# A two-block transformer in split fp32: one beginning, the expert loads, the window attention and four other places put in another order, and all weight splits ranked 60 instructions later

## The chip, the cores and the metric

The kernel runs on one core of a Trainium2 chip. The metric is the device time of one execution in microseconds (us). The engines are TensorE (PE in the profile, its weight loads PEld), VectorE (DVE), ScalarE (ACT), GpSimd (POOL) and SyncE (SP), which here issues most of the loads.

## What is computed

The reference is a transformer of two blocks on 256 tokens of width 1024, in fp32. Cut to its structure:

```
block 1:  x = LN_in(x)
          for l in 0, 1:
              m = MLA (8 heads) | differential (4) | forgetting (4) attention of x @ w_in[l]
              x = LN1(alpha * x + m @ w_out[l])
              x = LN2(alpha * x + MoE_l(x))     # 16 experts of width 512, 4 groups, top 2
block 2:  for i in 0, 1:
              x = x + FFN1_i(rms(x)) / 2
              x = x + (SSD scan and pooling mixer if i == 0 else sliding-window attention with sinks)
              x = x + cross-attention of rms(x) to a memory of 256 rows
              x = x + FFN2_i(rms(x)) / 2
```

## The kernel before

Tokens lie in two tiles of 128 rows, t = 0 and 1, in the rows tile `res`. A weight GEMM is made of three products of fp32r halves: each operand is split in a high part (an ACT copy to fp32r) and a low part (a DVE subtraction), and `mm3` (L479 to 485) adds high*high, high*low and low*high. `gemm_t` (L1618) does the same for transposed outputs, most of all in the FFN.

Weights come through the class `Stream` (L82 to 191). Its plan, fixed in `plan` and `plan2` (L331 to 477), is a list of 1 MB units that SP loads in that order into a ring of 7 stage tiles, and of pieces that are split from a unit into a ring of 6 piece tiles (L161 the ACT copy, L162 the DVE subtraction). Expert weights are `raw` units: used as plain fp32 and not split, they go to both rings in turn, or to a named free slot. `take` hands out a piece, `release` frees it and splits what comes next, `hold` stops the splitting ahead of a key, and `go` lifts that. Which instruction stands where on each engine is decided by the scheduler of the tile framework, which ranks instructions by the order in which the program traces them, and by priorities; `after(...)` lets an instruction stand behind named others.

**Block 1.** The beginning (`block1`, L775) loads x, small vectors, tables and the first units; `LayerNorm` (L194) normalizes rows (`ln_norm`, L570), and `x_t` (L534) transposes a tile on PE (L541) and splits it. There, gain and bias of the first LayerNorm are applied per column while PSUM is evacuated; the rows get theirs later (`ln_gain`, L598). `ln_full` (L584) does both on the rows, with gain and bias spread over the partitions. `mixer` (L818) runs five blocks of `w_in`, then the attentions; `fox_decay` (L1071) is the forgetting attention's decay. `memory` (L1715) prepares the normalized memory (L1724, L1729) for the cross-attention's keys and values, whose GEMM (`memory_gemm`, L1745) is done in quarters inside the MoE.

**MoE** (`moe`, L1208). Experts are taken in pairs, pr = 0 to 7, two experts side by side in the PE array. A pair has gate and up (`gate_or_up`, L1341, matmul L1352), activation (L1362, 1363), transposes (`tr`, L1369), down (L1386); `gather(g)` (L1306) collects the rows of two pairs, and `scatter` (L1401, residual add L1403) returns a pair's rows by a matmul with `ptr`. The tail after pair 7 is the last scatter, LN2 (L592 to 596) and the second half of the memory GEMM (L1758). A branch (L1410) handles overflow.

**Block 2.** `xattn` (L1805): queries (`queries`, L1821: squares, reciprocal root L506 to 518, scaling L1829 and L1831, transposes L1837, scores L1846), `attend` (L1849), output GEMM `xo`. `swa` (L1894), the window attention: first the keys and values of `qkv`, then `queries(0, 1)` and `queries(1, 1)` (L1946 to 1971, transposes L1967), then `attend(0)` and `attend(1)` (L1986) on eight score blocks (L1980, L1982; softmax from L2000, transposes L1150, L1168 out products), with the output GEMM `swo` behind. `ssd` (L2038): pooling input (L2059), rows (L2114), `bn` (L2145), the chain over heads (L2157 to 2181, prob L2163 and L2166, PE L2175), and z in eight blocks (L2189).

## Time and profile before

| | us |
|---|---|
| median of 3 runs (lowest, highest) | 2002.53 (2001.20, 2002.54) |
| the profiled execution's own time | 2002.3 |
| its span in the profile | 2000.5 |
| PE busy | 1935.0 (97%) |
| DVE busy | 1127.0 (56%) |
| ACT busy | 866.9 (43%) |
| DMA moved | 453.39 MB, mean 227 GB/s |
| mean granted clock of PE | 0.986 |

The span is the time from the first to the last instruction of one execution; the execution's own time has 1.8 us more around it. Busy time is a share of the whole span and says nothing about where an engine waits. PE's matmul ends are modelled, so a busy PE can still be at half its clock; the column PEclk of the windows table shows the clock granted in a stretch, where 1.00 is 2.4 GHz and 0.50 is 1.2 GHz. A row of the waits names the line that waited, after the arrow the engine, tile and line that it waited for, then the sum, the count and the longest in us.

### The profile page before, as it was taken

How to read it: one execution, taken by the hardware profiler on the slowest of the kernel's cores; microseconds unless marked ns; L12 is line 12 of the kernel's file. 1: busy time of each engine (PE TensorE's matmuls, PEld its weight loads, DVE VectorE, ACT ScalarE, POOL GpSimd, SP SyncE). 2: the span in 40 equal slices, each digit the busy share in tenths (PEclk: the TensorE clock that was granted, in tenths of full speed). 3: DMA queues.
4: the chain of work that ended last, by engine and by line, in shares of the span. 5: the costliest groups of instructions: out<-in, count | busy, mean ns of one | idle time of the engine just before them, and what ended most of it. 6: DMA issues, size and time to landing. Idle time of an engine off the chain costs nothing.

```text
span 2000.5 us, 28009 instructions
## 1 busy us (share of the span) xinstructions
PE 1935.0 (97%) x11069; PEld 1458.6 (73%) x11069; DVE 1127.0 (56%) x2211; ACT 866.9 (43%) x1539; POOL 58.0 (3%) x119
## 2 busy tenths in 40 slices
PE   6999999999999998899999899999999999999999
PEld 6776433367864333599988887899989986778998
DVE  7775122167751221656579775655665567766554
ACT  6563110136631101455466555644454455556443
POOL 1110000000100000000001000000000000000000
PEclk9999999999999999999999999999999997999999
DMA  8456999973569999855564353455555543335550
GB/s 290 145 203 229 397 419 420 421 256 123 206 236 403 420 421 421 300 187 181 186 202 137 132 219 109 163 190 190 190 200 186 182 165 137 127 99 175 190 190 22
DMA packets 176044, 453.39 MB, mean 227 GB/s; under 512 B 11120, under 2 KB 106844, under 8 KB 149148
## 3 DMA queue, kind: packets, MB, share of 16 engines
q1 hardware_dynamic: 172044, 435.55, 59.1%
q0 software_dynamic: 3856, 15.91, 2.2%
q8 instruction: 91, 1.49, 0.3%
q14 instruction: 53, 0.43, 0.1%
HBM read 446.19 MB, written 5.24 MB: 226 GB/s over the span
## 4 chain that ended last, share of the span: by engine, by line
PE 56%; DMA 5%; DVE 3%; ACT 2%; issue 0%; POOL 0%; DVEq 0%; SPq 0%; POOLq 0%; ACTq 0%
PE mm L1623 7%; PE mm L1625 7%; PE mm L1624 7%; PE accb L485 5%; PE accb L484 5%; PE accb L483 4%; PE acca L485 4%; PE acca L484 4%; PE acca L483 4%; DMA piece<-in_exp_w_gate_dram 2%; DMA piece<-in_exp_w_down_dram 1%; DMA stage<-in_exp_w_down_dram 1%; DMA stage<-in_exp_w_up_dram 1%; DVE piece L162 1%; PE mm L1876 1%; PE mm L541 1%
## 5 line engine op out<-in xcount | busy, mean ns | idle before, releaser
L162 DVE TENSOR_TENSOR piece<-stage,piece 128x1024 fp32r<-128x1024 f32 (+3 forms) x439 | 513.8, 1179 | 240.9 <-ACT piece L161 239.3
L161 ACT ACTIVATE piece<-stage 128x1024 fp32r<-128x1024 f32 (+3 forms) x439 | 444.5, 1021 | 343.8 <-PE mm L1625 204.4
L1352 PE MATMUL mm<-stage,m 128*64 128x512 f32 x512 | 221.8, 595 | 0.0
L1352 PE MATMUL mm<-piece,m 128*64 128x512 f32 x480 | 215.1, 596 | 2.0 <-DMA piece<-in_exp_w_up_dram 2.0
L1623 PE MATMUL mm<-m,piece 128*128 128x256 f32 x736 | 207.0, 281 | 2.3 <-DVE m L2189 2.3
L1624 PE MATMUL mm<-m,piece 128*128 128x256 f32 x736 | 206.7, 281 | 0.0
L1625 PE MATMUL mm<-m,piece 128*128 128x256 f32 x736 | 206.6, 281 | 0.0
L1623 PE MATMUL mm<-xh,piece 128*128 128x256 f32 x576 | 163.1, 283 | 0.0
L1625 PE MATMUL mm<-xh,piece 128*128 128x256 f32 x576 | 163.0, 283 | 0.0
L1624 PE MATMUL mm<-xl,piece 128*128 128x256 f32 x576 | 162.9, 283 | 0.0
L484 PE MATMUL accb<-piece,m 128*128 128x512 f32 (+1 forms) x364 | 144.3, 397 | 0.0
L485 PE MATMUL accb<-piece,m 128*128 128x512 f32 (+1 forms) x364 | 143.7, 395 | 0.5 <-DVE m L493 0.5
L483 PE MATMUL accb<-piece,m 128*128 128x512 f32 (+1 forms) x364 | 143.1, 394 | 0.9 <-ACT m L950 0.7
L1623 PEld LDWEIGHTS mm<-m,piece 128*128 128x128 f32 x736 | 139.4, 189 | 4.6 <-issue 3.0
L1624 PEld LDWEIGHTS mm<-m,piece 128*128 128x128 f32 x736 | 139.3, 189 | 1.9 <-issue 0.3
L1625 PEld LDWEIGHTS mm<-m,piece 128*128 128x128 f32 x736 | 139.4, 189 | 0.0
L483 PE MATMUL acca<-piece,m 128*128 128x512 f32 (+1 forms) x348 | 138.2, 398 | 0.2
L485 PE MATMUL acca<-piece,m 128*128 128x512 f32 (+1 forms) x348 | 137.2, 396 | 0.5 <-DVE m L493 0.5
L484 PE MATMUL acca<-piece,m 128*128 128x512 f32 (+1 forms) x348 | 137.7, 396 | 0.0
L1352 PEld LDWEIGHTS mm<-stage,m 128*64 128x64 f32 x512 | 65.1, 137 | 76.4 <-issue 73.8
L1623 PEld LDWEIGHTS mm<-xh,piece 128*128 128x128 f32 x576 | 110.4, 192 | 1.3
L1624 PEld LDWEIGHTS mm<-xl,piece 128*128 128x128 f32 x576 | 110.4, 192 | 1.2
(567 smaller groups left out, 3535.8 us busy)
## 6 DMA issues: line engine op xcount, KB each, us to landing
stage<-in_ffn_wi_dram SPq DMA_DIRECT2D x88, 1024.0 KB, 5.5
stage<-in_ffn_wo_dram SPq DMA_DIRECT2D x44, 1024.0 KB, 5.4
stage<-in_exp_w_down_dram SPq DMA_DIRECT2D x38, 1024.0 KB, 18.6
stage<-in_exp_w_up_dram SPq DMA_DIRECT2D x34, 1024.0 KB, 11.2
stage<-in_exp_w_gate_dram SPq DMA_DIRECT2D x30, 1024.0 KB, 18.5
piece<-in_exp_w_gate_dram SPq DMA_DIRECT2D x30, 1024.0 KB, 17.9
piece<-in_exp_w_up_dram SPq DMA_DIRECT2D x30, 1024.0 KB, 15.0
piece<-in_exp_w_down_dram SPq DMA_DIRECT2D x26, 1024.0 KB, 16.8
```

What stands on the lines that cost most here:

```text
L161: nc.scalar.activation(wh, src, AF.Copy)
L162: nc.vector.tensor_tensor(wl, src, wh.bitcast(F32), op=OP.subtract)
L483: nc.tensor.matmul(out, ah, bh, start=first, stop=False)
L484: nc.tensor.matmul(out, ah, bl, start=False, stop=False)
L485: return nc.tensor.matmul(out, al, bh, start=False, stop=last)
L541: self.moved = nc.tensor.transpose(p[:, k * P:(k + 1) * P], src[:, 4 * q + k:D:8], self.c["ident"])
L1352: mm = nc.tensor.matmul(o[64 * k:64 * k + 64, :], x[:, j, s:s + CAP], w[k][:, jj, :], start=(j == 0), stop=(j == 7))
L1623: nc.tensor.matmul(out, wh[:, j, :], hi[:, j, :], start=(j == 0), stop=False)
L1624: nc.tensor.matmul(out, wh[:, j, :], lo[:, j, :], start=False, stop=False)
L1625: nc.tensor.matmul(out, wl[:, j, :], hi[:, j, :], start=False, stop=(j == 7))
L1876: nc.tensor.matmul(po[:, k * P:(k + 1) * P], v[:, mc, h * 256 + cc * P:h * 256 + (cc + 1) * P], pt[t][:, (2 * h + mc) * P:(2 * h + mc + 1) ...
```

## The change

It joins several edits.

1. *Splits.* Both instructions of a weight split are traced under a priority of −60, so that the scheduler ranks them as if they came 60 instructions later. A raw unit in the piece ring waits only for the splits before it, and no longer for raw pieces.
2. *Beginning.* The first LayerNorm and LN1 apply gain and bias to the rows at once (`ln_full`), so `ln_norm`, `ln_gain`, the gain columns of both, and the bias branch of `x_t` are gone. Their vectors are loaded as rows, those of the first LayerNorm right after the first tile of x; the first unit of `w_in` is issued ahead of the small loads. Splitting starts with two pieces after tile 0's copies, the rest after tile 1's LayerNorm. The router's weights need no scaling any more.
3. *MoE.* Four expert halves that are not first in the stream are loaded early into slots that are free: up of expert 0 and both downs; before, two gate halves were. Gathers copy without gain; `gather(1)` comes at the end of pair 1, `ptr` in pair 2, gathers 2 and 3 in pairs 3 and 5. A pair's down stands behind its last up matmul. The second half's memory weights are loaded ahead of the next block's; in the tail splitting begins again only after LN2's tile 0 (two pieces) and tile 1.
4. *Mixer.* `fox_decay` stands after the MLA attention instead of after the third block of `w_in`; the differential heads' rotation goes from POOL to DVE.
5. *Cross-attention.* The query GEMM of t = 1 is finished bank by bank with its norm, transposes and scores come after the last query product, and the output weights are held until the last normalization of the attention.
6. *Window attention.* The order is queries 0, keys and values, attend 0, queries 1, attend 1.
7. *SSD.* Evacuations L2059, L2114 and L2145 go from DVE to ACT; z is copied by ACT and multiplied by DVE in SBUF.

The core of the diff:

```diff
+        self.ws = Stream(nc, self.sp, self.wp, self.slot, lambda: self.tc.high_priority(-60))
...
+            with self.later():
+                nc.scalar.activation(wh, src, AF.Copy)
+                nc.vector.tensor_tensor(wl, src, wh.bitcast(F32), op=OP.subtract)
...
-        self.units.append(dict(ap=ap, a=a, b=b, left=1, tile=None, ring=ring, slot=slot, first=len(self.pieces)))
+        first = max((p["n"] + 1 for p in self.pieces if not p.get("raw")), default=0)
+        self.units.append(dict(ap=ap, a=a, b=b, left=1, tile=None, ring=ring, slot=slot, first=first))
...
+            slots = {("up", 0, 4): "m4", ("down", 0, 0): "xl", ("down", 1, 0): "m1", ("down", 0, 4): "xh"}
...
+                    if n == NSTAGE + NPIECE - 2:
+                        early("down", 1, 0)
+                        early("down", 0, 4)
+            mem(1024 * l + 512)
...
-            mem(1024 * l + 512)
...
-                self.plan_cols("qkv", w, 1024, 512)
-                self.plan_cols("qkv", w, 0, 1024)
+                for c0 in (0, 1024, 512):
+                    self.plan_cols("qkv", w, c0, 512)
...
-        self.rsqrt1(r, mv[:, 1:2], 0)
-        nc.vector.scalar_tensor_tensor(v, v, r, gb[1], op0=OP.mult, op1=OP.add)
+        sqrt = self.rsqrt1(r, mv[:, 1:2], 0)
+        return sqrt, nc.vector.scalar_tensor_tensor(v, v, r, gb[1], op0=OP.mult, op1=OP.add)
...
+            if l == 0 and bi == 0:
+                with self.after(*norm.half):
+                    ws.go(2)
+                with self.after(norm.last, norm.sqrt):
+                    ws.go()
...
-                nc.scalar.activation(x[:, j0, :], p[:, 0:256], AF.Identity, scale=g1[:, j0:j0 + 1], bias=b1[:, j0:j0 + 1])
-                at = nc.vector.tensor_scalar(x[:, j0 + 1, :], p[:, 256:512], g1[:, j0 + 1:j0 + 2], b1[:, j0 + 1:j0 + 2],
-                                             op0=OP.mult, op1=OP.add)
+                nc.scalar.activation(x[:, j0, :], p[:, 0:256], AF.Copy)
+                nc.vector.tensor_copy(x[:, j0 + 1, :], p[:, 256:512])
...
-            prev = []
+            prev = [state["last"]]
...
-                if pr == 8:
-                    with self.after(state["silu"], state["tr"]):
-                        ws.go(4)
-            if pr == 0:
-                gather(1)
-            if pr == 1:
+            if pr == 2:
...
+            with self.after(*nxt.copied):
+                ws.go(2)
...
+        ws.hold("xo")
+        self.gemm_rows("xq", 8, lambda k: (hi[:, k, :], lo[:, k, :]), acc=rows(), done=chain, cuts=(2,), by_bank=True)
+        with self.after(self.last_mm):
+            for x in steps:
+                next(x, None)
...
+        with self.after(at[3]):
+            ws.go()
...
-        queries(0, 1)
-        queries(1, 1)
-        attend(0, bias, "xl")
+        attend(0, bias, "xl")
+        queries(1, 1)
...
-                nc.vector.tensor_scalar(u[:, t, b * 512:(b + 1) * 512], acc[t], r[:, t:t + 1], None, op0=OP.mult)
+                nc.scalar.activation(u[:, t, b * 512:(b + 1) * 512], acc[t], AF.Copy, scale=r[:, t:t + 1])
...
-            nc.vector.tensor_tensor(zs[:, ch, :], p[:, 0:256], rrow, op=OP.mult)
+            nc.scalar.activation(zs[:, ch, :], p[:, 0:256], AF.Copy)
+            nc.vector.tensor_tensor(zs[:, ch, :], zs[:, ch, :], rrow, op=OP.mult)
```

What this does to the order of instructions is shown at three places, before and after. A row has line, operation, out<-in and shape, and a count where it repeats. Lines of the changed kernel are its own.

DVE at the end of the second layer's MoE, before. L489 splits the last pair's rows, L1403 adds a scatter to the residual, L162 is a weight split, and L592 begins LN2.

```order
L489 TENSOR_TENSOR xh<-acca,xh 128x512 x2
L1403 SCALAR_TENSOR_TENSOR res<-res,mm 128x512 x4
L489 TENSOR_TENSOR xh<-accb,xh 128x512 x2
L1403 SCALAR_TENSOR_TENSOR res<-res,mm 128x512
L162 TENSOR_TENSOR piece<-stage,piece 128x1024 x2
L1403 SCALAR_TENSOR_TENSOR res<-res,mm 128x512
L162 TENSOR_TENSOR piece<-stage,piece 128x1024 x2
L1403 SCALAR_TENSOR_TENSOR res<-res,mm 128x512 x2
L592 BN_STATS bnst<-res 128x6 x3
```

The same place after, where L493, L1367, L167 and L577 are those lines.

```order
L493 TENSOR_TENSOR xh<-acca,xh 128x512 x2
L1367 SCALAR_TENSOR_TENSOR res<-res,mm 128x512 x4
L493 TENSOR_TENSOR xh<-accb,xh 128x512 x2
L1367 SCALAR_TENSOR_TENSOR res<-res,mm 128x512 x4
L577 BN_STATS bnst<-res 128x6 x3
L578 BN_AGGR bnmv<-bnst 128x2
L577 BN_STATS bnst<-res 128x6
L579 SCALAR_TENSOR_TENSOR res<-res,bnmv,gv 128x1024
```

The two pairs of weight splits no longer stand among the residual adds.

DVE in the first cross-attention, before: the query norm of t = 0, from the variance of the four heads (L512) to the scaling of the products (L1831).

```order
L162 TENSOR_TENSOR piece<-stage,piece 128x1024
L514 RECIPROCAL sq_t<-sq_t 128x4
L162 TENSOR_TENSOR piece<-stage,piece 128x1024
L515 TENSOR_TENSOR sq_v<-sq_v,sq_t 128x4
L516 TENSOR_TENSOR sq_v<-sq_v,sq_t 128x4
L162 TENSOR_TENSOR piece<-stage,piece 128x1024
L517 TENSOR_SCALAR sq_v<-sq_v 128x4
L518 TENSOR_TENSOR xss<-sq_v,sq_t 128x4
L162 TENSOR_TENSOR piece<-stage,piece 128x1024
L1829 TENSOR_SCALAR xss<-xss,rms_r 128x4
L162 TENSOR_TENSOR piece<-stage,piece 128x1024
L1831 TENSOR_TENSOR m_12447<-acca,xss 128x512 x2
```

After, L516 to L522 are the same helper, and L1795 is the scaling.

```order
L516 TENSOR_SCALAR sq_v<-xssq 128x4
L518 RECIPROCAL sq_t<-sq_t 128x4
L519 TENSOR_TENSOR sq_v<-sq_v,sq_t 128x4
L520 TENSOR_TENSOR sq_v<-sq_v,sq_t 128x4
L521 TENSOR_SCALAR sq_v<-sq_v 128x4
L522 TENSOR_TENSOR xssq<-sq_v,sq_t 128x4
L1793 TENSOR_SCALAR xssq<-xssq,rms_r 128x4
L1795 TENSOR_TENSOR m_12376<-acca,xssq 128x512 x2
```

Between the links of the chain stood five splits (L162), and none stands there now.

PE in the window attention, before: the last query products (L483 to L485), the first scores (L1980, L1982) and the transposes of the second half's queries (L1967).

```order
L484 MATMUL accb<-piece,m_16266 128x512
L485 MATMUL accb<-piece,m_16267 128x512
L1980 MATMUL acca<-m_16394,m_16392 128x128 x2
L1982 MATMUL acca<-m_16394,m_16392 128x256 x2
L1980 MATMUL acca<-m_16394,m_16392 128x128 x2
L1982 MATMUL acca<-m_16394,m_16392 128x256
L1967 MATMUL mm<-ident,xh 128x128 x8
L1982 MATMUL acca<-m_16394,m_16392 128x256
L1980 MATMUL acca<-m_16394,m_16392 128x128
L1982 MATMUL acca<-m_16394,m_16392 128x256
L1980 MATMUL acca<-m_16394,m_16392 128x128
L1982 MATMUL acca<-m_16394,m_16392 128x256
```

After, L1961 and L1963 are the scores, L486 to L488 the query products of the second half, and L1948 the transposes of the keys.

```order
L1948 MATMUL mm<-ident,m_16334 128x128 x8
L487 MATMUL accb<-piece,m_16207 128x512
L488 MATMUL accb<-piece,m_16208 128x512
L486 MATMUL accb<-piece,m_16207 128x512
L1961 MATMUL acca<-m_16335,m_16333 128x128 x2
L1963 MATMUL acca<-m_16335,m_16333 128x256 x2
L487 MATMUL accb<-piece,m_16207 128x512
L488 MATMUL accb<-piece,m_16208 128x512
L1961 MATMUL acca<-m_16335,m_16333 128x128
L1963 MATMUL acca<-m_16335,m_16333 128x256
L1961 MATMUL acca<-m_16335,m_16333 128x128
L1963 MATMUL acca<-m_16335,m_16333 128x256
```

The scores now stand between products of the second half's queries; before, all products stood ahead of them.

## Rows read from the trace of the kernel before

**Rows 1.** page part 1: engine, busy us, share of span, instructions

```profile
PE 1935.0 (97%) x11069; PEld 1458.6 (73%) x11069; DVE 1127.0 (56%) x2211; ACT 866.9 (43%) x1539; POOL 58.0 (3%) x119
```

**Rows 2.** longest waits of PE: line waited for, total us, times, longest

```profile
PE accb L483 <- ACT xh L488: 4.7, 1, 4.7
PE acca L1980 <- DVE wnm L2000: 4.5, 2, 4.2
PE mm L541 <- DVE sq_y L530: 4.0, 1, 4.0
...
PE tp L2175 <- DVE prob L2166: 3.4, 2, 2.3
PE mm L1837 <- DVE m L1831: 3.2, 2, 1.6
PE accb L483 <- ACT gv L966: 2.5, 1, 2.5
PE mm L1623 <- DVE m L2189: 2.3, 1, 2.3
PE mm L1724 <- DVE m L1729: 2.2, 1, 2.2
PE accb L1386 <- DMA stage<-in_exp_w_down_dram: 2.1, 2, 1.3
PE mm L1352 <- DMA piece<-in_exp_w_up_dram: 2.0, 2, 1.3
...
PE accb L1758 <- DMA stage<-in_mem_wkv_dram: 1.4, 1, 1.4
```

**Rows 3.** windows: stretch, us, busy of PE, PEld, DVE, ACT, POOL; PEclk; DMA

```profile
44.50:51.30 6.80, 5.13 (x19) 3.94 (x19) 5.97 (x36) 5.58 (x11) 1.02 (x4) 0.50 0.60 203
225.00:400.00 175.00, 168.05 (x741) 64.19 (x738) 39.69 (x61) 17.96 (x30) 4.19 (x12) 1.00 1.01 420
407.40:413.70 6.30, 3.35 (x10) 1.70 (x10) 6.26 (x9) 3.29 (x5) 0.00 (x0) 0.95 1.06 371
413.10:416.50 3.40, 3.40 (x6) 1.65 (x6) 3.40 (x8) 0.00 (x0) 0.00 (x0) 0.50 1.07 372
822.70:826.10 3.40, 2.94 (x10) 2.42 (x11) 2.41 (x6) 2.83 (x7) 0.00 (x0) 0.50 1.09 380
1112.80:1119.70 6.90, 4.64 (x25) 4.28 (x22) 5.53 (x11) 1.58 (x4) 0.00 (x0) 0.51 0.62 223
1676.00:1703.30 27.30, 25.82 (x85) 16.31 (x85) 14.25 (x78) 13.17 (x45) 0.00 (x0) 0.50 0.10 37
```

**Rows 4.** part 5 of the page: both instructions of a weight split

```profile
L162 DVE TENSOR_TENSOR piece<-stage,piece 128x1024 fp32r<-128x1024 f32 (+3 forms) x439 | 513.8, 1179 | 240.9 <-ACT piece L161 239.3
L161 ACT ACTIVATE piece<-stage 128x1024 fp32r<-128x1024 f32 (+3 forms) x439 | 444.5, 1021 | 343.8 <-PE mm L1625 204.4
```

**Rows 5.** timeline of DVE, end of the second MoE: start, us, line

```profile
809.72 2.35 DVE L162 TENSOR_TENSOR piece<-stage,piece 128x1024 fp32r<-128x1024 f32 x2
...
812.59 2.35 DVE L162 TENSOR_TENSOR piece<-stage,piece 128x1024 fp32r<-128x1024 f32 x2
```

**Rows 6.** timeline of PE, MoE 0, pair steps in a row and alone

```profile
248.81 0.59 PE L1352 MATMUL mm<-piece,m 128*64 128x512 f32 x1
...
249.24 0.59 PE L1352 MATMUL mm<-piece,m 128*64 128x512 f32 x1
...
260.63 1.07 PE L1352 MATMUL mm<-stage,m 128*64 128x512 f32 x2
```

**Rows 7.** timeline of DVE, cross-attention 0, query norm

```profile
1206.85 1.23 DVE L162 TENSOR_TENSOR piece<-stage,piece 128x1024 fp32r<-128x1024 f32 x1 [0.78 <-ACT piece L161]
...
1212.30 1.23 DVE L162 TENSOR_TENSOR piece<-stage,piece 128x1024 fp32r<-128x1024 f32 x1
```

**Rows 8.** timeline of DVE, SSD, first z evacuation

```profile
1114.96 0.42 DVE L2189 TENSOR_TENSOR m<-mm,w 128x256 f32<-128x256 f32 x1
```

**Rows 9.** timeline of DVE, window attention before its first softmax

```profile
1668.52 2.35 DVE L162 TENSOR_TENSOR piece<-stage,piece 128x1024 fp32r<-128x1024 f32 x2
```

More of the change, by code (lines that the diff above doesn't have):

```diff
@@ L217, in tile @@
             if t == 0:
-                self.hh = k.slot("m5", F32R).rearrange("p (t j f) -> p t j f", t=2, j=8)
-                self.hl = k.slot("m2", F32R).rearrange("p (t j f) -> p t j f", t=2, j=8)
-            v = self.res[:, t, :].rearrange("p (f j) -> p j f", j=8)
-            self.parts = k.split(v, self.hh[:, t], self.hl[:, t])
+                return
+            self.hh = k.slot("m5", F32R).rearrange("p (t j f) -> p t j f", t=2, j=8)
+            self.hl = k.slot("m2", F32R).rearrange("p (t j f) -> p t j f", t=2, j=8)
+            with k.after(self.sqrt, self.last):
+                for i in range(2):
+                    v = self.res[:, i, :].rearrange("p (f j) -> p j f", j=8)
+                    k.split(v, self.hh[:, i], self.hl[:, i])
         else:
@@ L224, in tile @@
                 self.hi, self.lo = k.xt(self.tags[0]), k.xt(self.tags[1])
-            self.copied = k.x_t(self.res[:, t, :], t, self.hi, self.lo, self.g, self.b)
-    def gain(self, gb=None):
-        for t in range(2):
-            self.k.ln_gain(self.res, t, gb or self.gb)
+            self.copied = k.x_t(self.res[:, t, :], t, self.hi, self.lo, self.g)
+            if t == 0:
+                self.half = self.copied
+            self.moved = k.moved
 class RmsNorm:
@@ L484, in mm3 @@
         nc.tensor.matmul(out, ah, bl, start=False, stop=False)
-        return nc.tensor.matmul(out, al, bh, start=False, stop=last)
+        self.last_mm = nc.tensor.matmul(out, al, bh, start=False, stop=last)
+        return self.last_mm
     def split(self, src, hi, lo):
@@ L816, in block1, with mixer @@
         return res, ln
-    def mixer(self, l, norm, res, steps=None, moe=None):
+    def mixer(self, l, norm, res, steps=None):
         nc, I, c, ws = self.nc, self.I, self.c, self.ws
@@ L891, in mixer @@
         if l == 0:
-            with self.after(at[1]):
-                norm.gain()
             late(at, steps[0])
@@ L1210, in moe @@
         n, hh, hl = ln.n, ln.hh, ln.hl
[L1211 to L1214 removed]
+        ws.free.append("m1")
         sc = self.sm(32, "gsc")
@@ L1357, in gate_or_up @@
                 ws.release(2)
+            state["last"] = mm
             return o
```

280 lines of the change are left out of this document (119 added, 161 removed).

## Prediction

> **What bounds the kernel now.** I read four views, from coarse to fine. The first is the page's table of engines [rows 1]. TensorE (PE) is busy 1935.0 us of a span of 2000.5 us, so it waits for 2000.5 − 1935.0 = 65.5 us in all; VectorE (DVE) is at 56% and ScalarE (ACT) at 43%. A change of order can win little more than those 65.5 us, unless it makes PE's busy time itself shorter. The second view says who made PE wait [rows 2]. The waits are many and short. Nearly all are for DVE or ACT at the joints between stages, and a few for expert weights. The long FFN stages do not appear: there PE never stops, and nothing is to be had. The third view, the windows table [rows 3], has what the waits do not show: the granted clock. Five of its stretches run at 0.50 or 0.51, that is at 1.2 instead of 2.4 GHz; each begins where PE waited or had only small matmuls in the stretch before. PE is "busy" in them, but does half the work. The longest is the window attention, 1676.0 to 1703.3. If its 25.82 busy us were run at the full clock they would need about half, so up to 12.9 us lie there besides the waits. The fourth view is of single instructions on DVE at these joints [rows 5, 7 to 9]: the short chain for which PE waits has weight splits between its links.
>
> A split is one ACT copy and one DVE subtraction, 439 of each, mean 1.02 and 1.18 us [rows 4], so together 2.2 us for a piece of weights. DVE's idle time before a subtraction is nearly all for ACT's copy (239.3 of 240.9 us), and ACT's before a copy mostly for a matmul that frees a piece (204.4 of 343.8 us). So splits mostly run as soon as a buffer is free, well ahead of use. They can be moved back without PE running dry, except where all the room in the ring comes free late.
>
> The sum is made against the profiled execution, 2002.3 us, 0.2 us under the median of the runs shown (2002.53 us).
>
> **Weight splits ranked later.** The work is the same; only places change. This pays at the joints priced below, and is counted there. What it costs is counted last.
>
> **The beginning.** LayerNorm now puts gain and bias on the rows, where it left them to the evacuation of the transposes and to four row passes later. The first tile's chain needs two vector loads and a longer last instruction; the first weight unit is fetched earlier, and the eight gain steps per tile are gone. PE's wait for the first split transposes was 4.7 us [rows 2]. I take +1 us of gain, bounds −2 (the loads of gain and bias delay everything) and 4.7.
>
> **First mixer.** PE waits 2.5 us for L966 (the forget-gate decay) and 2.2 us for L1729 (the memory keys), and a stretch of 6.8 us follows the second of them at half clock, 5.13 us of it busy [rows 2, 3], worth 5.13 / 2 = 2.6 us. Ceiling 7.3 us. The four row passes on DVE are gone and the decay chain moved behind the first attention. But the norm of the memory, for which L1729 waits, stays. I take 4; bounds −2 and 7.3.
>
> **MoE, weights.** DMA moves 420 GB/s at a share of 1.01 from 225 to 400 us [rows 3], so the expert stream can't go faster, only start sooner. Four half-experts now sit in free slots, the first gate tiles all come from the rings, and the ring is free for the next load some steps earlier. PE's DMA waits with rows are 2.1 + 2.0 + 1.4 = 5.5 us in both layers [rows 2], each of them at most 1.4 us long. A start a few us earlier removes them all: 5.5, bounds 0 and 5.5.
>
> **MoE, pair steps.** In a row, pair steps stand 0.43 us apart (248.81 to 249.24); one that stands alone among transposes takes 1.07 us, where one matmul takes 0.59 [rows 6], so leaving a run costs about 0.48 us. PE's new order has about six fewer such breaks in each layer, 2 × 6 × 0.48 = 5.8 us at most. I take 3.5, bounds 0 and 5.8, since some of those breaks only wait for what then waits elsewhere.
>
> **MoE, ends.** At the end of layer 1 DVE's order has two pairs of splits between the last residual adds (first order fences), 809.72 and 812.59 with 2.35 us each [rows 5], 4.7 us in all; PE then waits 4.0 us for the LayerNorm behind them and runs on at half clock, 2.94 us busy [rows 2, 3]: 4.0 + 1.5 = 5.5. At layer 0 the stretch 407.4 to 413.7 has 6.30 − 3.35 = 2.95 us of idle PE, and then 3.40 us at half clock [rows 3]: 2.95 + 1.7 = 4.7. In the new order no split stands there, and the memory weights come before the next block's. What is late next is the first split of the block after the MoE, counted below. I take 8 of 10.2, bounds 4 and 10.2.
>
> **Cross-attention.** PE waits 3.2 us in two places for L1831, the query scaling [rows 2]. Its chain of small DVE steps has five splits between its links, from 1206.85 to 1212.30, at 1.23 us each [rows 7]; the new order has none there, because the output weights are held (second order fences). The chain then ends several us sooner. I take 3, bounds 0 and 3.2.
>
> **SSD.** PE waits 3.4 us for L2166 and 2.3 us for L2189, and 4.64 us are busy at half clock from 1112.8 [rows 2, 3]: 3.4 + 2.3 + 2.3 = 8.0. Three kinds of PSUM evacuation go from DVE to ACT, which unloads DVE there. But z costs one instruction more: the ACT copy, and then the multiplication in SBUF, which from PSUM took 0.42 us at 1114.96 [rows 8]. I take 5, bounds 0 and 8.0. On this the Trainium skill speaks against the change: "VectorE: DVE Perf Modes", section "Rules for kernel authors", would have one accept the slower read from PSUM for an elementwise step on a matmul's result, and copy to SBUF first only if many operations follow. Here one follows. By that rule the eight z blocks get longer and the SSD's gain is nearer to its lower bound; no row of before shows the copied form.
>
> **Window attention.** Queries of the first half now come before the keys, so the second half's query products stand among the first scores as filler (third order fences). Four splits no longer stand ahead of the first softmax, two of them in one row of 2.35 us [rows 9]. PE waited 4.5 us there [rows 2], and half clock costs up to 12.9. Ceiling 17.4. The filler is one block of 48 products, of which only some 18 are left when the scores begin, so it can't carry the whole stretch: the clock will fall later, or for less long. I take 9, bounds 2 and 17.4.
>
> **New waits.** After a hold the splits start together when it is lifted: at the first block behind each MoE and at both output projections of the cross-attention, four places. There PE may wait for a piece, one split of 2.2 us [rows 4] or two. I take 1 us a place, −4; bounds 0 and 4 × 4.4 = 17.6.
>
> The sum: 1 + 4 + 5.5 + 3.5 + 8 + 3 + 5 + 9 − 4 = 35 us. 2002.3 − 35 = 1967.3, and with the 0.2 us to the median 1967.5.
>
> **The rivals.** (a) *Only the waits go, the clock stays.* PE gets the work sooner but still has only small matmuls at the joints. Then of the terms are left: weights 5.5, ends 4.0 + 2.95 = 7, cross-attention 3, SSD's first wait 3, window attention 4.5, less 4 of new waits: 19 us, 1983.5. For it: 25.82 us of the half-clock stretch are busy, with little idle time in it that a new order could close [rows 3]. Against it: filler was moved exactly there.
>
> (b) *The clock holds.* The window attention runs through (17.4 instead of 9), the SSD too (8 instead of 5), and the held pieces are in time (0 instead of −4): 35 + 8.4 + 3 + 4 = 50 us, 1952.5. For it: each low stretch is entered from a wait named above.
>
> (c) *The expert stream binds.* At a share of 1.01 the early loads only change which tile is late, and the order of steps saves nothing: without 5.5 + 3.5 us it is 1976.5. Against it: PE is busy 168.05 of 175.00 us in that stretch [rows 3].
>
> (d) *Slower: PE runs dry.* A subtraction that is ranked behind DVE's other work comes too late for the first piece of a GEMM, and PE waits 2.2 us, one split. The gains without new waits are 39 us, so from 18 such waits on the change loses. There are about 30 weight GEMMs outside the MoE; if each begins so, 66 us are lost and the time is 2002.5 − 39 + 66 = 2029.5. Against it are ACT's and DVE's shares and the ring of six pieces [rows 1, 4].
>
> **How the numbers follow.** Forecast 0.44, (a) 0.20, (b) 0.18, (c) 0.11, (d) 0.07. Whether the change does what it says is no rival: the orders show it. The range reaches from (b), a little further down for the other ceilings, to (a), a little further up for more waits on pieces: 1949 to 1988. Outside are (d) and the tails of the others. A measurement of this kernel tells about 0.2%, 4 us, from no change. The first four cases lie under that bound but for their tails: faster 0.88, same 0.05, slower 0.07.
>
> **What would show it.** Right: no wait for L530 after the second MoE, a DMA wait sum in the MoE near zero, none for L1831 in cross-attention, and a half-clock stretch in the window attention well under 27 us. Wrong: waits of PE for L162's subtraction or L161's copy in a list where none stands now, above all at the first FFN block and at the output projections; half clock at new places; or a busy sum of PE that stays near 1935 us, which would mean that only idle time was won.

## The result, and the profile after

The changed kernel takes 1946.79 us (median; 1945.82 to 1946.95), against 2002.53 us before: a ratio of 0.9722, 95% interval 0.9705 to 0.9739. The gain is 55.7 us. The forecast was 1967.5 us, a gain of 35, and its range ended at 1949: the direction was right, the size too small, and the time lies 2.2 us below the range. The profiled execution took 1946.73 us with a span of 1944.9.

The page of the changed kernel: the span, the engines, and the granted clock in 40 slices.

```profile
span 1944.9 us, 27901 instructions
...
PE 1905.3 (98%) x11029; PEld 1443.2 (74%) x11029; DVE 1118.8 (58%) x2226; ACT 863.3 (44%) x1550; POOL 46.6 (2%) x93
...
PEclk9999999999999999999999999999999999999999
```

PE's busy time fell from 1935.0 [rows 1] to 1905.3 us, and its idle time from 65.5 to 1944.9 − 1905.3 = 39.6 us. So only 26 of the 56 us were idle time, and 30 us came out of busy time. The work is nearly the same (11029 matmul records against 11069). Most of the 30 us is the clock. Before, the trace has seven stretches at half clock: the five of [rows 3], and two to which the prediction gave no term (columns as there):

```profile
64.90:68.40 3.50, 2.96 (x7) 2.38 (x8) 3.21 (x17) 1.30 (x5) 0.00 (x0) 0.51 1.03 418
184.40:187.80 3.40, 3.40 (x12) 1.53 (x14) 0.43 (x3) 0.00 (x0) 0.00 (x0) 0.50 0.93 348
```

PE is busy for 48.3 us in the seven. In the changed kernel two are left, with 6.4 us:

```profile
564.80:568.20 3.40, 3.40 (x12) 0.96 (x10) 0.00 (x0) 0.00 (x0) 0.00 (x0) 0.50 0.53 210
1643.40:1646.80 3.40, 2.99 (x13) 1.98 (x13) 2.85 (x13) 3.17 (x11) 0.00 (x0) 0.50 0.80 294
```

Reckoned as in the prediction, half of such time is lost: 24.1 us before and 3.2 after. By this estimate some 21 us of the gain are clock, and about 9 us are busy time that became shorter at the full clock, some 6 of them in the bodies of the MoEs. The stretch at 564.8 us, at MoE 1's start, is at a new place; the one at MoE 0's start (184.4) is gone.

PE's longest waits in the changed kernel:

```profile
PE mm L545 <- DVE res L581: 12.1, 1, 12.1
PE mm L1132 <- DVE prob L1997: 3.9, 3, 2.5
PE mm L545 <- DVE sq_y L534: 2.6, 2, 1.3
PE accb L1813 <- ACT m L1806: 1.8, 2, 0.9
PE accb L1350 <- PEq L1375: 1.6, 1, 1.6
PE accb L486 <- ACT piece L166: 1.4, 1, 1.4
PE mm L1365 <- DVE res L1367: 1.3, 4, 0.3
PE accb L487 <- DVE piece L167: 1.1, 1, 1.1
```

Of the waits in [rows 2], those for expert weights, for L1831's query scaling, for the SSD's chain and for the forget gate's vector are gone. But where the query scaling was waited for, the scores (L1813) now wait for the copies of the transposed queries (L1806), 2.9 us in both cross-attentions, of which 1.8 stand in the row above; the like wait was 0.6 us before. And LN2 behind the MoE still costs 1.3 us in each layer (L534). L1132 is a transpose of softmax rows, that is the place in the window attention that was L1980's before. L545's 12.1 us are the beginning, where 7.2 stood before. Two waits are for weight pieces (L486 and L487); they too stand in the beginning.

The stages, taken between PE's own marks in the two traces (the first and last matmul of a kind), in us. The last column is the term of the prediction, cut to the stage; the 8 us for the MoE's ends are shared out by their ceilings, 4.7 and 5.5.

| stage | before | after | change | predicted |
|---|---|---|---|---|
| span's start to first expert product | 185.0 | 177.6 | −7.4 | −5 |
| MoE 0, first gate to last down | 221.9 | 213.9 | −8.0 | −3.8 |
| MoE 0's end and second mixer | 178.7 | 172.3 | −6.4 | −3.7 |
| MoE 1, first gate to last down | 221.7 | 213.6 | −8.1 | −3.8 |
| MoE 1's end to the first FFN's transposed products | 49.2 | 44.4 | −4.8 | −5.7 |
| first FFN and pooling input | 218.6 | 217.7 | −0.9 | 0 |
| SSD, up to its last z | 56.4 | 50.1 | −6.3 | −5 |
| SSD's output and cross-attention 0 | 150.4 | 148.4 | −2.0 | −1.5 |
| window attention and cross-attention 1 | 210.4 | 199.2 | −11.2 | −10.5 |
| new waits, spread over four places | | | | +4 |
| the rest | 508.2 | 507.7 | −0.5 | 0 |

### The profile page after: what moved, and what is told of

It is laid out like the page before. It is cut to its first block, busy times and chain, and to the rows that moved or that the text cites. A ratio compares the mean times of both kernels' runs of the same rounds, so it can differ in the third digit from the quotient of the medians.

```text
span 1944.9 us, 27901 instructions
## 1 busy us (share of the span) xinstructions
PE 1905.3 (98%) x11029; PEld 1443.2 (74%) x11029; DVE 1118.8 (58%) x2226; ACT 863.3 (44%) x1550; POOL 46.6 (2%) x93
## 4 chain that ended last, share of the span: by engine, by line
PE 61%; ACT 2%; DVE 2%; issue 0%; POOL 0%; ACTq 0%; DVEq 0%
PE mm L1585 8%; PE mm L1587 8%; PE mm L1586 8%; PE acca L487 5%; PE acca L488 5%; PE acca L486 4%; PE accb L487 4%; PE accb L486 4%; PE accb L488 4%; PE mm L1315 3%; PE accb L1350 1%; PE acca L1350 1%; PE mm L1849 1%; ACT piece L166 1%; PE mm L545 1%; PE mm L1365 1%
## 5 line engine op out<-in xcount | busy, mean ns | idle before, releaser
L167 DVE TENSOR_TENSOR piece<-stage,piece 128x1024 fp32r<-128x1024 f32 (+3 forms) x439 | 513.5, 1179 | 237.7 <-ACT piece L166 236.2
L1315 PE MATMUL mm<-stage,m 128*64 128x512 f32 x528 | 231.0, 599 | 0.0
L486 PE MATMUL accb<-piece,m 128*128 128x512 f32 (+1 forms) x364 | 143.3, 394 | 1.4 <-DVE res L1668 0.8
L487 PE MATMUL accb<-piece,m 128*128 128x512 f32 (+1 forms) x364 | 144.5, 397 | 0.0
L488 PE MATMUL accb<-piece,m 128*128 128x512 f32 (+1 forms) x364 | 144.3, 396 | 0.0
L486 PE MATMUL acca<-piece,m 128*128 128x512 f32 (+1 forms) x348 | 137.3, 395 | 0.9 <-ACT m L496 0.8
L487 PE MATMUL acca<-piece,m 128*128 128x512 f32 (+1 forms) x348 | 137.6, 396 | 0.0
L488 PE MATMUL acca<-piece,m 128*128 128x512 f32 (+1 forms) x348 | 137.1, 395 | 0.0
```

Of the source, the lines that this page charges most:

```text
L167: nc.vector.tensor_tensor(wl, src, wh.bitcast(F32), op=OP.subtract)
L486: nc.tensor.matmul(out, ah, bh, start=first, stop=False)
L487: nc.tensor.matmul(out, ah, bl, start=False, stop=False)
L488: self.last_mm = nc.tensor.matmul(out, al, bh, start=False, stop=last)
L1315: mm = nc.tensor.matmul(o[64 * k:64 * k + 64, :], x[:, j, s:s + CAP], w[k][:, jj, :], start=(j == 0), stop=(j == 7))
```

## The experiments

"a_" kernels are the changed kernel with one thing put back, "b_" kernels the one before with one thing added. The kernel before, timed beside each group, had medians from 1999.57 to 2002.76 us. A ratio is to that.

### Is it the rank?

`a_rank0` gives the priority block the value 0:

```diff
-lambda: self.tc.high_priority(-60)
+lambda: self.tc.high_priority(0)
```

> The changed kernel with the splits' priority back at 0, all else kept. Theory R (the rank is a minor part; the joints were cleared by the hold, the moved calls and the evacuations on ACT): 1947 to 1952 us. Theory S (the rank is what keeps splits out of the DVE chains at the joints, so it carries a third or more of the 56 us): 1962 to 1970 us, with waits of PE for LayerNorm or query scaling back.

`b_rank60` puts the block around the two split instructions of the kernel before and changes nothing else.

```diff
-            nc.scalar.activation(wh, src, AF.Copy)
-            nc.vector.tensor_tensor(wl, src, wh.bitcast(F32), op=OP.subtract)
+            with self.later():
+                nc.scalar.activation(wh, src, AF.Copy)
+                nc.vector.tensor_tensor(wl, src, wh.bitcast(F32), op=OP.subtract)
```

> The kernel before with nothing but both split instructions ranked 60 later. Theory R: 1998 to 2004 us. Theory S: 1980 to 1988 us, with the waits for L530, L1831 and L2000 gone. Rival (d) of the prediction (late splits starve PE): above 2006 us, with new waits for L162.

`a_norank` has no block at all (the diff above, in the changed kernel and the other way round), since the value 0 moved instructions too.

> The changed kernel with the splits traced without any priority block (the block with priority 0 also moved instructions, so it was no clean removal). If the rank is worth what the first run showed: 1953 to 1956 us. If the block itself was the disturbance: 1947 us, as the changed kernel.

`a_rank120` doubles the rank:

```diff
-lambda: self.tc.high_priority(-60)
+lambda: self.tc.high_priority(-120)
```

> The changed kernel with the splits ranked 120 instead of 60 later. If the joints are clear already and later splits only bring new waits: 1950 us or more, with waits for L167 where none stands now. If there was still something to clear: 1940 to 1944 us.

Measured: 1954.01 us (0.9761, 0.9743 to 0.9779), 1991.07 (0.9943, 0.9924 to 0.9962), 1954.37 (0.9768, 0.9753 to 0.9783) and 1948.32 (0.9743, 0.9730 to 0.9756). So the rank is worth 7.6 us in the changed kernel and 10.6 alone. That is between the two theories: not a third of the gain, and not negligible. By stages, without it the window attention's stage is 3.5 us longer, MoE 0's end and the second mixer 2.0 and the first FFN 1.5. In the kernel before the rank alone shortens the SSD from 56.4 to 48.9, as much as the whole change does there, and makes MoE 1's end longer (50.7 against 49.2), since the splits fall back into LN2's chain: four stand there, from 809.81 us on, 4.62 us in all. So most of its 10.6 us are the SSD's 7.5, and the waits that its expectation names are not gone: PE waits 8.1 us for the LayerNorm (L532 there), 3.2 for the query scaling (L1833) and 4.0 at the first scores of the window attention. Rival (d) has no support: ranked 120 later, the kernel isn't told from the changed one, the time lies between the two that its expectation names, and PE's waits for L167 are small (1.8 and 1.3 us in all, of which 1.1 stand in the changed kernel's beginning too).

### The MoE's body

`a_oldslots` loads two gate halves early, as before, instead of the four others:

```diff
-slots = {("up", 0, 4): "m4", ("down", 0, 0): "xl", ("down", 1, 0): "m1", ("down", 0, 4): "xh"}
+slots = {("gate", 0, 0): "xl", ("gate", 1, 0): "m4"}
```

> The changed kernel with the two early gate halves of before instead of the four early up and down halves; the new places of the gathers are kept. If the lead of the expert stream made the MoE bodies shorter: 6 to 9 us slower than the changed kernel (1953 to 1956 us), with 6 us of DMA waits back in both layers. If the order of steps did it: at most 2 us slower, no DMA waits.

`a_oldmoe` also puts the gathers and `ptr` back:

```diff
-            if pr == 1:
-                gather(1)
...
-            if pr == 2:
+            if pr == 0:
+                gather(1)
+            if pr == 1:
                 ptr.append(...)
-            if pr in (3, 5):
+            if pr in (2, 4):
```

> As the run with the old early halves, and gather 1, ptr and gathers 2 and 3 also at their old places (pairs 0, 1, 2, 4). If the lead of the stream is all: the same time as that run. If the places of the gathers carry part of it: 3 to 8 us more than that run, up to 1962 us, in which case pair steps are broken up again.

Measured: 1956.37 us (0.9775, 0.9756 to 0.9793) and 1958.88 (0.9789, 0.9770 to 0.9808). The bodies of the two MoEs, 213.9 and 213.6 us in the changed kernel, take 216.6 and 218.1 with the old slots and 217.0 and 221.7 with both. The waits of PE in MoE 1's body, first with the old slots, then with both:

```profile
PE mm L1362 <- DVE xh L490: 2.4, 1, 2.4
PE acca L1347 <- PEq L1372: 1.1, 1, 1.1
PE mm L1362 <- DVE res L1364: 0.6, 2, 0.3
```

```profile
PE accb L1347 <- DMA stage<-in_exp_w_down_dram: 2.5, 2, 1.3
...
PE acca L1347 <- DMA piece<-in_exp_w_down_dram: 0.9, 1, 0.9
PE mm L1312 <- DMA piece<-in_exp_w_up_dram: 0.4, 1, 0.4
```

With the old slots alone no DMA wait is left, against the expectation of 6 us, and yet the bodies are 7.2 us longer: neither of the two theories fits. PE's busy time is 2.8 and 2.3 us longer there (214.07 and 213.80 us), and 2.4 us are the wait for a pair's split rows (L490). With both edits, 2.5 + 0.9 + 0.4 = 3.8 us of DMA waits are back, as many as in the kernel before. MoE 1 is then as long as before, but MoE 0 still 4.9 us shorter; no run takes that apart (the down products behind the last up matmul and the gathers without gain were not tried alone).

The windows of the two bodies, before and after (columns as in [rows 3]):

```profile
185.00:406.90 221.90, 214.95 (x970) 83.49 (x970) 46.11 (x74) 24.77 (x42) 4.19 (x12) 0.99 0.97 399
585.60:807.30 221.70, 213.60 (x969) 84.45 (x969) 45.78 (x72) 24.82 (x42) 4.03 (x5) 1.00 0.98 402
```

```profile
177.60:391.50 213.90, 211.26 (x971) 82.80 (x970) 44.40 (x74) 22.73 (x42) 4.18 (x12) 1.00 0.99 413
563.80:777.40 213.60, 211.49 (x970) 82.93 (x969) 44.08 (x72) 22.73 (x42) 3.98 (x5) 0.99 0.99 413
```

PE's busy time is 3.7 and 2.1 us shorter for the same number of matmuls. PE's longer waits in MoE 1's body, before:

```profile
PE accb L1386 <- DMA stage<-in_exp_w_down_dram: 2.1, 2, 1.3
PE acca L1386 <- PEq L1411: 1.4, 1, 1.4
PE mm L1401 <- DVE res L1403: 1.1, 3, 0.5
PE acca L1386 <- DMA piece<-in_exp_w_down_dram: 1.0, 1, 1.0
PE tp L1369 <- DVE prob L1363: 0.9, 1, 0.9
PE mm L1352 <- DMA piece<-in_exp_w_up_dram: 0.7, 1, 0.7
```

In the changed kernel's MoE 1 two such waits are left, 1.1 us for the overflow branch (PEq) and 0.6 for the residual add (L1367). So the 16.1 us of the two bodies come apart as follows. Waits for expert weights were 2.5 us in MoE 0 and 3.8 in MoE 1, and all 6.3 are gone. Waits for DVE (the residual add behind a scatter, the activation, the gathered rows) are 2.0 us shorter in each, 4.0 in all. Busy time is 5.8 us shorter; the clock has no share in that sum, since MoE 0's start won 1.7 us by it (1.4 of them inside the body's marks) and MoE 1's start lost 1.7. So about 6 us of busy time became shorter at the full clock.

What fits this is the order of steps. I counted the places where PE goes from one kind of step to another (gate or up, down, transposes, gather, scatter): 67 before and 53 after in MoE 0, 63 and 49 in MoE 1, and 61 and 59 with old slots and gathers. A count gives no price by itself, because the time at a change holds the next step's ordinary time as well, and two changes, away and back, make one break of a run. That these changes carry the 6 us is argued from the order and not shown by a run that moves nothing else.

### The MoE's ends

`a_oldtail` releases the splits behind the MoE as before:

```diff
+                if pr == 8:
+                    with self.after(state["silu"], state["tr"]):
+                        ws.go(4)
...
-            with self.after(*nxt.copied):
-                ws.go(2)
```

> The changed kernel with the splits behind the MoE released as before (four pieces at pair 8, none at LN2's first tile). DVE then has four splits inside LN2's chain. If their place is what cost the time at the MoE's ends: 2 to 4 us more in each layer, 1950 to 1954 us, with a wait for the LayerNorm of 3 us or more back. If the first GEMM behind the MoE had been waiting for late pieces: a little faster, 1945 us.

`a_norank_oldtail` is this edit and that of `a_norank` together.

> The changed kernel without the rank and with the old release of splits behind the MoE. If the old release is only harmful together with the rank: 1954 to 1957 us. If it costs by itself, as in the run with the old release: 1966 to 1970 us, both MoE ends 5 us longer than without the rank.

`b_tail` makes only this edit (and the order of the memory weights) in the kernel before.

> The kernel before with only the release of splits behind the MoE moved (two pieces after LN2's first tile, the rest after the second) and the memory weights loaded ahead of the next block's. If the ends of the MoE are worth what the run with the old release showed: 10 to 13 us faster than before (1989 to 1992 us), both stages shorter by 5 or more. By the sum of the prediction (8 + 1.4 us, less 2 for new waits): 1994 to 1996 us. If the rank is needed for it: 1999 to 2002 us.

Measured: 1962.39 us (0.9803, 0.9783 to 0.9823), 1970.68 (0.9849, 0.9833 to 0.9865) and 1999.98 (0.9976, 0.9958 to 0.9993). With the old release the changed kernel loses 15.6 us, the most of all edits: MoE 0's end and the second mixer 6.4, MoE 1's end 5.3 (2 to 4 in each were expected), and MoE 1's body 3.9, where PE is busy for 8.5 us at half clock instead of 3.4 (about 2.6 us) and waits 1.84 us for a pair's split rows (L493) ahead of a scatter. It loses as much without the rank (16.3), so the release counts by itself. DVE at MoE 1's end with the old release, and then PE there:

```profile
797.60 2.36 DVE L167 TENSOR_TENSOR piece<-stage,piece 128x1024 fp32r<-128x1024 f32 x2
...
801.13 2.35 DVE L167 TENSOR_TENSOR piece<-stage,piece 128x1024 fp32r<-128x1024 f32 x2
...
803.66 1.28 DVE L581 SCALAR_TENSOR_TENSOR res<-res,lnr,gv 128x1024 f32<-128x1024 f32 x1
```

```profile
792.08 7.03 PE L1721 MATMUL accb<-stage,m 128*128 128x512 f32 x16
805.00 1.33 PE L545 MATMUL mm<-ident,res 128*128 128x128 f32 x5 [5.89 <-DVE res L581]
```

Two pairs of splits stand inside LN2's chain, the first row is normalized at 804.9, and PE waits 5.89 us for it behind the memory's products. In the changed kernel the same place on PE reads:

```profile
777.91 2.81 PE L1365 MATMUL mm<-xh,xl 128*128 128x512 f32 x8
780.55 7.03 PE L1720 MATMUL accb<-stage,m 128*128 128x512 f32 x16
788.91 1.16 PE L545 MATMUL mm<-ident,res 128*128 128x128 f32 x8 [1.33 <-DVE sq_y L534]
789.90 7.03 PE L1720 MATMUL accb<-piece,m 128*128 128x512 f32 x16
796.77 1.05 PE L545 MATMUL mm<-ident,res 128*128 128x128 f32 x8
797.57 0.48 PE L486 MATMUL acca<-piece,xh 128*128 128x512 f32 x1
```

Scatter, the first half of the memory's GEMM, 1.33 us of wait, tile 0's transposes, the second half, tile 1's, and the next block: the first pieces were split under the second half, and no wait for them shows. So the cost charged for late pieces did not come. `b_tail` is less clear. Its profile has MoE 0's end shorter by 2.0 and MoE 1's by 4.7, but its ten runs fall in groups: four of 1990.6 to 1991.3 us at a granted clock of 0.989, one of 1998.5 at 0.987, and five of 2001.5 to 2002.3 at 0.984 or 0.985. The profile is of a run of 2001.9 us, and what the ends gain there, other stages lose again (the beginning 1.8 us, MoE 1's body 2.1, the SSD 1.5). What the edit alone gains in the kernel before is not settled by it.

### The window attention

`a_oldswa` has the old order, with the weights' order to it:

```diff
-        queries(0, 1)
         acc = self.gemm_block("qkv", hi, lo, 0)
...
-        attend(0, bias, "xl")
+        queries(0, 1)
         queries(1, 1)
+        attend(0, bias, "xl")
```

> The changed kernel with the window attention in its old order (keys and values first, then both query halves, then both attends). If the order supplies filler that keeps the clock: 6 to 9 us slower than the changed kernel (1953 to 1956 us) and a half-clock stretch of 20 us or more back in that stage. If the gain there came from splits leaving the chain: at most 2 us slower.

`a_norank_oldswa` is this edit and that of `a_norank` together, so that DVE's order around the first softmax is that of before.

> The changed kernel without the rank and with the window attention's old order, so that DVE has five splits (L162's) around the second query half again, as before. If order and rank do the same work there and either is enough: 5 to 8 us above the run without the rank (1954.4), 1959 to 1963 us, with 17 us or more of half clock in that stage. If it is only a matter of when the clock recovers: runs scattered between 1953 and 1963 us, the granted clock of each going with its time.

Measured: 1948.15 us (0.9726, 0.9703 to 0.9748; runs from 1944.06 to 1950.86) and 1961.1 (0.9801, 0.9787 to 0.9816; 1956.61 to 1962.55). The second is 6.7 us above the kernel without the rank, the first not to be told from the changed kernel. The stage takes 199.2 us with both order and rank, 199.8 with the rank alone, 202.7 with the order alone and 208.3 with neither, one execution each; PE is busy in it at half clock for 3.0, 8.3, 5.4 and 25.5 us, against 25.8 in the kernel before. So in the changed kernel order and rank do much the same work, and either is enough for most of it. The forecast had put the term down to the filler.

But the rank does not always do it. `b_rank60` has the rank and the old order too, and its stage takes 208.2 us. Part of that is the cross-attention, which has no hold there. The rest shows how far the clock goes its own way: `b_rank60` and `a_oldswa` have the same order in the window attention, 292 instructions of PE in a row and 322 of DVE, from before the first score to after the last. Counted from the end of the FFN ahead of it (1614.2 us in the one, 1582.6 in the other), PE's instructions start within 0.07 us of each other for 63 us, and then part; at the end they are 4.8 us apart. Three windows of 10 us, from about 50 us after that FFN, of `b_rank60` and then of `a_oldswa`:

```profile
1664.20:1674.20 10.00, 5.67 (x26) 4.24 (x26) 8.84 (x38) 8.36 (x28) 0.00 (x0) 0.77 0.62 211
1674.20:1684.20 10.00, 9.53 (x29) 5.81 (x29) 4.24 (x22) 2.42 (x8) 0.00 (x0) 0.50 0.00 0
1684.20:1694.20 10.00, 9.99 (x48) 6.18 (x47) 5.69 (x29) 4.89 (x20) 0.00 (x0) 0.71 0.00 0
```

```profile
1632.50:1642.50 10.00, 5.68 (x26) 4.26 (x26) 8.82 (x38) 8.36 (x28) 0.00 (x0) 0.72 0.62 210
1642.50:1652.50 10.00, 9.53 (x47) 5.64 (x47) 5.98 (x32) 4.14 (x15) 0.00 (x0) 0.77 0.01 2
1652.50:1662.50 10.00, 9.99 (x56) 6.32 (x55) 7.00 (x36) 5.93 (x24) 0.00 (x0) 1.00 0.00 0
```

The first rows are alike to the instruction count, at clocks of 0.77 and 0.72. Then the clock stays at 0.50 through the second window in the one and rises in the other. By PEclk the low time is 20.4 us in the first kernel and 10.2 in the second; half of the difference is 5.1 us, near the 4.8. In the changed kernel:

```profile
1629.10:1639.10 10.00, 10.00 (x57) 7.02 (x57) 8.08 (x39) 9.19 (x31) 0.00 (x0) 1.00 0.00 0
1639.10:1649.10 10.00, 6.84 (x29) 4.51 (x27) 8.84 (x28) 8.75 (x24) 0.00 (x0) 0.83 0.32 107
1649.10:1659.10 10.00, 8.83 (x54) 5.45 (x52) 6.13 (x31) 4.58 (x16) 0.00 (x0) 1.00 0.28 105
```

3.4 us at half clock are left. PE's idle time in the whole stage hardly changed, 8.0 us before and 7.6 after: the wait of 4.5 us for L2000 is gone, and 3.9 us for the softmax (L1997) stand in its place. So what the stage gained is the clock.

### The SSD

`a_oldssd` has the four evacuations on DVE again; of z:

```diff
-            nc.scalar.activation(zs[:, ch, :], p[:, 0:256], AF.Copy)
-            nc.vector.tensor_tensor(zs[:, ch, :], zs[:, ch, :], rrow, op=OP.mult)
+            nc.vector.tensor_tensor(zs[:, ch, :], p[:, 0:256], rrow, op=OP.mult)
```

> The changed kernel with the four SSD evacuations back on DVE (z multiplied straight from PSUM). If the evacuations on ACT made the SSD's gain: 4 to 7 us slower (1951 to 1954 us). If ranking the splits later is enough by itself there, as the stage of the kernel before with nothing but the rank suggests (48.9 us from the pooling GEMM to the last z, against 56.4): within 1.5 us of the changed kernel, and by the skill's rule for one elementwise step even a little faster.

`a_rank0_oldssd` is this edit and that of `a_rank0` together.

> As the run with the SSD's old evacuations, and the splits' priority at 0 too. If the two edits do the same work in the SSD, so that either is enough: 1959 to 1962 us, that is 5 to 8 us above the run with the rank at 0 alone (1954.0). If the new SSD gains nothing by either: 1953 to 1955 us.

`a_simple` is this edit and that of `a_oldswa` together.

> The changed kernel with both the window attention's old order and the SSD's old evacuations. If the rank makes both edits needless: 1945 to 1949 us, not to be told from the changed kernel. If each covers for the other: 1953 us or more.

Measured: 1945.42 us (0.9717, 0.9697 to 0.9737), 1956.74 (0.9780, 0.9761 to 0.9801) and 1948.99 (0.9747, 0.9733 to 0.9760; runs from 1943.27 to 1953.54). The SSD's stage takes 49.0 us with the old evacuations, against 50.1 in the changed kernel. So they win nothing beside the rank. Nor is it z that makes the 1.1 us: they are a wait of PE ahead of z for ACT (0.97 us at 1045.6, for L2087), and in z PE waits in neither kernel. The Trainium skill ("VectorE: DVE Perf Modes", section "Rules for kernel authors") would have one accept the read from PSUM where only one elementwise step follows. The rows agree as far as they go: the multiplication takes 0.42 us from SBUF (L2170) as from PSUM (L2169 in `a_oldssd`), and the copy on ACT comes on top with 0.36 to 0.39 us; but the stage's length does not decide it.

With the value 0 the old evacuations cost 2.8 us (52.0 against 49.2), less than the 5 to 8 expected; two waits of 1.72 us for the heads' chain (L2146) come back. So either the rank or the new evacuations are enough for these 3 us. The other 4.4 us up to 56.4, about as much as the wait for z (2.3) and the half clock (2.3) of before, did not come back, and which edit removed them is open.

### The cross-attention's hold

`a_nohold` drops the hold:

```diff
-        ws.hold("xo")
...
-        with self.after(at[3]):
-            ws.go()
```

> The changed kernel without the hold on the cross-attention's output weights (bank by bank and late transposes are kept). If the hold keeps splits out of the query norm: 2 to 4 us slower (1949 to 1951 us), with 1.6 us of waits for L1831's successor back at each place. If the rank does it anyway: within 1 us, and the waits for ACT's and DVE's piece at the output projection (1.4 and 1.1 us) gone.

Measured: 1951.66 us (0.9745, 0.9730 to 0.9760). Both stages with a cross-attention are longer, by 2.3 and 2.5 us: 4.8 of a total of 4.9 us. The first is then 150.6 us long, as before the change (150.4). The waits of 1.4 and 1.1 us that the expectation puts at the output projection stand in the beginning, at 15.44 and 17.23 us.

### The beginning

`a_first2` splits the first two pieces ahead of tile 0's copies, `a_first2_oldssd` adds the old SSD:

```diff
         self.ws.limit = 0
+        self.ws.go(2)
...
-                with self.after(*norm.half):
-                    ws.go(2)
...
+            with k.after(*k.ws.acts if len(k.ws.acts) == 2 else ()):
+                self.copied = k.x_t(self.res[:, t, :], t, self.hi, self.lo, self.g)
```

> The changed kernel with the first two weight pieces split ahead of the first tile's copies instead of behind them. In the changed kernel ACT stands idle from 5.3 to 13.2 us and PE's first GEMM begins at 15.4, then waits until 17.2 for the second half of the first piece. If that release is what made the beginning late: the stage up to the first expert 1.5 to 2.5 us shorter, 1944 to 1946 us. If the weights land too late for it, or tile 0's copies are delayed by as much: 1946 to 1948 us.

> Both edits that looked better than, or as good as, the changed kernel: the first two pieces early and the SSD's old evacuations. If they add up: 1942 to 1945 us. If the first edit gives nothing: 1945 to 1947 us.

Measured: 1953.54 us (0.9757, 0.9740 to 0.9775) and 1954.2 (0.9766, 0.9749 to 0.9783). PE in the changed kernel, and then in `a_first2`:

```profile
12.05 1.97 PE L545 MATMUL mm<-ident,res 128*128 128x128 f32 x8 [12.05 <-DVE res L581]
15.44 0.69 PE L486 MATMUL accb<-piece,xh 128*128 128x384 f32 x1 [1.42 <-ACT piece L166]
17.23 0.69 PE L487 MATMUL accb<-piece,xh 128*128 128x384 f32 x1 [1.11 <-DVE piece L167]
```

```profile
14.42 0.69 PE L487 MATMUL accb<-piece,xh 128*128 128x384 f32 x1 [0.50 <-ACT xh L493]
...
20.78 1.16 PE L546 MATMUL mm<-ident,res 128*128 128x128 f32 x8 [1.50 <-DVE res L582]
```

The first product begins 1.0 us earlier, as wanted, but PE then waits 1.50 us for the second tile's LayerNorm, and up to the experts the kernel is 3.3 us slower. About 2.5 us of that are clock: 5.0 us at 0.50, most of it from 49.6 us on, behind waits for the norm of the memory (L1691), where the changed kernel has none. An earlier start of PE did not make that stage shorter, and there is no version here that beats the changed kernel by more than the measurement tells.

## Why the prediction was wrong in its size

**What bounds the kernel.** Right as far as it went: the gains lie at the joints and in the MoE, and the FFNs gave nothing (151.3 and 153.5 us as before). It said that little beyond the 65.5 us of idle time could be won unless busy time itself got shorter; 30 of 56 us came from there, about 21 by the clock and 9 at the full clock. The prediction had named both the clock and the breaks between steps, and took both too low.

**The beginning and the first mixer.** Predicted 1 + 4, measured 7.4. The sign at the very start was wrong: PE's first product came at 15.4 us instead of 13.9, since DVE waited 3.4 us for the gain's rows. Its first products also stand 0.32 us apart and only later 0.17, until 17.2 us before and until 22 or 23 us after, so the full rate comes some 5 us later. The mixer behind it made up for that and more: no wait for L966's or L1729's successors, and no half clock after 22 us, at a ceiling of 7.3. Which of the edits there gave how much was not tried.

**MoE, weights and pair steps.** This is the step that failed most: 16.1 us measured in the two bodies, where the prediction had 4.1 of its 5.5 (the other 1.4 are in the tail) and 3.5, that is 7.6. The weights were right in mechanism, but left out the short rows: 6.3 us of DMA waits were there and went. PE's waits for DVE inside the bodies, 4.0 us, were put at nothing. The breaks of pair steps were taken at 60% of their bound, and about 6 us of busy time went, which is the bound (5.8).

**MoE, ends.** Predicted 8 and 1.4, measured 6.4 + 4.8 = 11.2 with the second mixer in it. Right in mechanism, as the old release shows, but not all of the waits went: 1.3 us for LN2 are left in each layer.

**Cross-attention.** Predicted 3; measured 2.0 and 2.9 between its first transposes and the next FFN, 4.9 in all, and 4.8 by the run without the hold. That is above the ceiling of 3.2, although not all of the wait was won: at the first place 1.6 us went and 1.4 for L1806 came. There 1.0 us is idle time and 1.0 busy time, and the cause of the rest is open.

**SSD.** Predicted 5, measured 6.3. Right in size, but not for its reason: beside the rank the evacuations on ACT win nothing, and the rank alone does as much in the kernel before.

**Window attention.** Predicted 9, measured 8.4 without the cross-attention. Right in size, and partly by luck: of the wait of 4.5 us next to nothing was won, and of the 12.9 us of half clock 11.4 by the prediction's own reckoning, more than the term and more than the stage gained; what took the difference back is open. The filler is one of two causes.

**New waits.** Predicted 4 us of loss; no wait for a piece was measured at the four places. The pieces were split in time, as the trace at MoE 1's end shows. This and the MoE's bodies (16.1 where 7.6 was predicted) are 12.5 of the 21 us by which the sum fell short; the rest lies mostly in the beginning, the second mixer and the cross-attention.

Rival (b), without that cost and with the clock held, came nearest with 1952.5, but not in its own way: the window attention and the SSD stayed under the ceilings that it gave them. Rivals (a), (c) and (d) fall: the clock rose, no wait for the expert stream is left in the bodies, and PE does not run dry.

The lower end of the range was put a little under (b), at a gain of 53 us, where the ceilings of all terms together allowed 62. Terms that the prediction had not at all, the waits for DVE in the bodies and the half clock at 64.9 and 184.4 us, came on top.

## What to carry to other kernels

Where a scheduler fills an in-order queue, background work (here the splitting of weights) lands between the links of short chains for which the main engine waits. Here an explicit release after the chain was worth 15.6 us at the MoE's ends and a hold 4.9 us in the cross-attentions; ranking the splits later, by itself, cleared only the SSD. With the rank in place, some edits at single joints were needless (the SSD's evacuations, and most of the window attention's order). Read off a bottleneck engine's busy time what of it runs at half clock, and count the changes between kinds of steps in the new order: both are part of "busy". And list all waits of a stage that is to get shorter, the short ones and those for another engine too: in the MoE they made the largest miss.

## What the runs showed of the hardware

The granted clock came back at different times under the same instructions: 20.4 or 10.2 us at half clock with 292 matmuls and transposes in the same order, whose starts had agreed within 0.07 us until then. It shows in the totals, too. Five runs of one kernel (`a_simple`) went from 1943.27 us at a mean clock of 0.998 through 1948.80 at 0.995 to 1953.54 at 0.992. A loss of 0.006 of clock is 2 × 0.006 × 1950 = 23 us at half clock and should cost half of that, 11.7 us; 10.3 were measured. The changed kernel's four runs lie within 1.1 us at 0.997 to 0.999. Whether the new order of the window attention makes the clock depend less on chance is not shown by so few runs.

In the MoE's bodies the two matmuls of a pair step start 0.01 us apart and the next pair 0.42 to 0.43 us later; from a pair to a transpose, gather or scatter it is 0.52 us, 0.10 more. A pair step that stands alone takes 1.07 us for its two matmuls against 0.59 in a row [rows 6].
